# Four edits to the instruction order and buffer placement of a one-core transformer layer: where the feed-forward operands lie, who sums sequence 2's first weights, and what the table splits and casts stand behind

## The chip, the core and the metric

The kernel runs on one core of one Trainium2 chip. Its time is device microseconds of that core. Before the change the median of three runs is 2102.57 us (2102.38 to 2103.07). Engines are named as the profile names them: PE multiplies matrices (PEld is its weight load), DVE is VectorE, ACT is ScalarE, POOL is GpSimd, and SP issues most of the transfers.

## The reference, cut to what matters

Two sequences of 1024 rows and 1024 columns go through one encoder layer. Each has its own conditioning vector, from which six modulation vectors come.

```
h   = rmsnorm(x, g_mix) * (1 + sc1) + sh1
z   = h @ w_in                                 # query latent 256, key/value latent 128, rotary key 64, Fourier input 512
y1  = attention(latents), 4 heads              # full softmax over 1024 keys
y2  = real(fft2(Fourier input)) @ w_four       # over rows and over 64 columns in 8 groups
x   = x + ga1 * (concat(y1, y2) @ w_out)
h2  = rmsnorm(x, g_ffn) * (1 + sc2) + sh2
x   = x + ga2 * ((silu(h2 @ w_gate) * (h2 @ w_up)) @ w_down)     # inner width 2816
out = rmsnorm(x, g_final)
```

All of it is float32 in and out. The kernel keeps float32's accuracy by splitting each operand into a high and a low part: a cast on ACT gives the high part, a subtraction on DVE the low part, and three matmuls (high by high, high by low, low by high) replace one. The helper `split` (lines 62 and 63) is that cast and that subtraction, and `mm3` (lines 78 to 80) is the three matmuls. So nearly every operand passes ACT and DVE before PE can use it.

## The kernel before, in words

**Stages.** Stage 1 walks over eight pairs of row blocks (`pair`, four of each sequence). A pair normalizes and transposes its rows (`norm`, `flip`), multiplies them by the latent weights (`zproj`), transposes the latents (`latents`) and multiplies sums and differences of rows by the folded Fourier weights (`fourier_in`, `evenodd`). Behind the last pair the cosine table `tb[0]` is split. Stage 2 does the Fourier transform over rows (`dft`) with the cosine table `tb[0]` and the sine table `tb[1]`, and multiplies by the output weights that `prep_wm` casts (`fourier_out`). Stage 3 is attention: 64 items, each of one sequence, a block of 256 rows, a head and a half block (`scores`, `flip_p`, `values`), with the next block's queries (`load_q`, `rope_q`, `absorb_q`) and the output projection of an earlier block (`out_step`, `out_proj`, `norm2`, `flip_h`) between them. Stage 4 is the feed-forward part.

**The feed-forward part.** Its products are done by a seven-product scheme of two-by-two blocks: seven combinations of the four blocks of an operand, seven products, and sums of products. `prep_h` splits the seven combinations of h2 (`H[0]`, `H[5]` and so on) into resident tiles, two for each (`H00` and `H01` are the high and the low part of combination 0). `combos(n)` loads the gate and up weights of inner block n into a tile `rgu` and `sums_w` makes their combinations by four subtractions, t3, b12, t2 and t4, all on POOL except for the first two of sequence 1. The loop over n runs seven steps `step(j, ...)`, each a product of twelve matmuls; after step j the weight combination j of the next n is split by `hl` (a `wh` and a `wl` tile, eight buffers of each). The products add up in three banks x, y, z, which `nc.scalar.copy(p1, x)` (line 1397), `add(u2, y, p1, ...)` and later sums read (their helper is line 138). Behind that, `prod2` multiplies by the down weights, and `rows_out` normalizes and stores output rows as a list of seven small steps; for sequence 1's last rows that list is `pending`, and sequence 2's loop over n takes a step from it at two places in each n.

**What sets the order.** The order in each engine's queue is written by a scheduler while the kernel is built. It takes the source order, looks ahead, and is bound by explicit marks: `tc.issue_after(i)` keeps what stands inside it behind instruction i on its engine, `behind()` does so for the cast and the subtraction of the last `split`, and `first(early, late)` sets one order. Within an engine the instructions then run in that order, and one that waits holds all behind it.

**Where tiles lie.** A pool hands out addresses in the order in which tags are first asked for. Stage 4's resident tiles (pool `p5`, tags such as `H00`, `H41`, `X0`, `X1`) are laid over the memory of stage 3. A tile can be written only when the last reader of what lay there has finished. In the kernel before, tag `H41` lies over stage 3's `lat01` (last used by `comb_h`'s result) and tag `H00` over `ckv0` and `ckv1`, the values that the last `values` reads. `H41` first serves as `wc`, the target of the first four weight sums.

**The tail of stage 3.** After the last item, `out_proj(1, 2, ...)` alternates with the last `flip_p` and `values`. Then `out_proj(1, 3, ...)` and two norms and transpositions run between `prep_h`'s steps, ahead of the first feed-forward product. The two `gb` banks that `out_proj` and `values` share come free by DVE (line 938 adds the projection to `x2`).

Of the kernel before, what the change touches and what calls it, by code (L numbers as in the profile page):

```python
# [16 lines left out]
ALU = mybir.AluOpType  # L17
# [35 lines left out]
def hybrid_encoder_kernel(ctx: ExitStack, tc: tile.TileContext, a: dict):  # L53
    nc = tc.nc

    here = {}
# [4 lines left out]
    def split(hi, lo, src):  # L61
        here["a"] = nc.scalar.copy(hi, src).ins  # L62
        here["v"] = nc.vector.tensor_tensor(out=lo, in0=src, in1=rd(hi), op=ALU.subtract).ins  # L63
# [100 lines left out]
    with ExitStack() as st:  # L164
# [378 lines left out]
        def pair(k):  # L543
            if k == 0:
                return first_pair()
            zproj(k, 0)
            if k + 1 < nk:
                flip(k + 1, 0)
                flip(k + 1, 1)
            next(more, None)  # L550
            zproj(k, 1)
            latents(k, 0)
            if k + 1 < nk:
                flip(k + 1, 2)
                flip(k + 1, 3)
            if k + 2 < nk:
                x_load(k + 2)
            next(more, None)
            fourier_in(k, 0)
            latents(k, 1)  # L560
            next(more, None)
            fourier_in(k, 1)
            if k + 1 < nk:
                evenodd(k + 1)
            if k + 2 < nk:
                norm(k + 2)
# [12 lines left out]
        raws = {}  # L579
# [3 lines left out]
                nc.sync.dma_start(raws[k, c][:, :n], a["tcos" if k == 0 else "tsin"][:, c, :])  # L583
        tb[0] = [wr.tile([P, 4, NT], F32R, name=f"tb0{i}") for i in range(2)]
        pair(nk - 1)
        for c in range(4):
            split(tb[0][0][:, c, :], tb[0][1][:, c, :], raws[0, c])

    S = {}

# [106 lines left out]
    with ExitStack() as st:  # L697
# [149 lines left out]
        zsplit(0)  # L847
        nyq_split()
        tb[1] = [wa.tile([P, 4, 512], F32R, name=f"tb1{i}") for i in range(2)]
        for c in range(4):  # L850
            split(tb[1][0][:, c, :], tb[1][1][:, c, :], raws[1, c][:, :512])
        abn = dft(0)
        prep_wm(0)
        zsplit(1)
        scT = wa.tile([P, NC, 32], F32, name="scT2")
        nc.sync.dma_start(scT, sc_d)
# [23 lines left out]
        for s in range(2):  # L880
            for j in (1, 2, 3, 0):
                with tc.issue_after(S.pop("ld")) if (s, j) == (1, 1) else ExitStack():
                    fourier_out(s, abn, j)
                if (s, j) == (1, 1):
                    gate_wo(1, None, here["st"])
                if s == 1 and j == 2:
                    ex = tiny.tile([P, 1], F32, name="ex")
                    nc.vector.memset(ex, 0.0)
                    with tc.issue_after(here["a"]):
                        nc.scalar.activation(ex, ex, AF.Exp)  # L890
                    for u in range(2):
                        rope_q(0, 0, u, bank2)
                if s == 1 and j == 3:
                    absorb_q(0, 0, 0, bank2)
                    for u in range(2):
                        rope_flip(0, 0, u, bank2t)
                if s == 0:
                    n = (1, 2, 3, 0).index(j)
                    mod2(2 * n)
                    mod2(2 * n + 1)  # L900
            if s == 0:
                mr = wa.tile([P, 512], F32, name="modrow2")
                nc.vector.tensor_copy(mr, chunks.pop("ps"))
                abn = dft(1)
                prep_wm(1)
                mod_vecs(mr, bank2, bT, gT, 24, 1, s2, sh2)
                early.close()
                E3 = ExitStack()
                e = E3.enter_context(tc.tile_pool(name="p3e", bufs=1, side="left", reuse_waits="tile"))
                wq_h, wq_l, rc, rs = stage3_loads(gate_wo, rd(abn[1][1][:, 1, 0:1]))  # L910
# [65 lines left out]
    with ExitStack() as st:  # L976
# [104 lines left out]
        for k in range(nit + 4):  # L1081
            if k >= nit:
                i = k - nit
                out_proj(1, 2, i // 2, i % 2)
                S["tail", i] = here["v"]
                if i == 1:
                    norm2(1, 2, 0, tl)
                    S["tail", 5], S["tail", 6] = here["n"]
            if k < nit:
                s, b, h, u = items[k]  # L1090
                scores(s, b, h, u)
                nxt = items[k + 8 - k % 8] if k + 8 - k % 8 < nit else None
                i = k % 8
                if nxt is not None:
                    if i == 0:
                        load_q(*nxt[:2])
                    if i == 3 and nxt[1] == 0:
                        load_seq(nxt[0], w)
                    if i in (3, 4):
                        rope_q(*nxt[:2], i - 3, gbank)  # L1100
                    if i in (5, 6):
                        rope_flip(*nxt[:2], i - 5, tbank)
                if u == 1 and k + 1 < nit:
                    absorb_q(*items[k + 1][:3], gbank)
            if 0 <= k - 1 < nit:
                flip_p(*items[k - 1])
                if k == nit:
                    S["tail"] = here["a"], here["v"]
            if 0 <= k - 3 < nit and (k - 3) % 2 == 1:
                values(*items[k - 3][:3])  # L1110
                if k == nit + 2:
                    S["tail", 4], S["tail", 7] = here["v"], here["a"]
            m = k - 11
            if 0 <= m < 8 * NOUT:
                out_step(*divmod(m // 8, 4), m % 8)
                if m % 8 in (1, 3) and k + 1 < nit:
                    S["late"] = here["n"][1]
            for f in todo.get(k, ()):
                f()

    with ExitStack() as st:
# [6 lines left out]

        def quad(tag, dt=F32):
            return w.tile([P, 4, 512], dt, tag=tag, name=tag, bufs=1)  # L1130

        def prep_h(H, s, n):

# [147 lines left out]
        for s in range(2):  # L1281
            def combos(n, first=False):
                f = order[n]
                if first and n == 1:
                    b = [val() for _ in range(4)]
                    for i, t in enumerate(b):
                        nc.sync.dma_start(t, a["wgu"][i // 2, f][:, 4 * (i % 2) : 4 * (i % 2) + 4, :].rearrange("p c m -> p (c m)"))
                    return b
                r = w.tile([P, 2, 1024], F32, tag=f"X{n % 2}", name="rgu", bufs=1)
                for i in range(2):  # L1290
                    nc.sync.dma_start(r[:, i, :], a["wgu"][i, f])
                return sums_w([r[:, 0, :512], r[:, 0, 512:], r[:, 1, :512], r[:, 1, 512:]], lambda i: val(), nc.gpsimd)

            def comb_h(s, c):
                a11, a21, a12, a22 = (val() for _ in range(4))
# [64 lines left out]
            for n, f in enumerate(order):  # L1360
# [10 lines left out]
                def step(j, ps, k, first, src=src):  # L1371
                    prod(ps, k, cur[j], first)
                    if s == 0 and n == 0:
                        if j == 0:
                            cur.extend(hl(v) for v in w0[4:])
                            w0.clear()
                            norm3(1, S.pop("jk3").bitcast(BF16))
                        if j < 3:
                            with behind():
                                for _ in range(2):  # L1380
                                    next(prep, None)
                            return
                        if j == 3:
                            src = S["w1"] = sums_w(src, lambda i: val(), nc.vector)
                        src = S["w1"]
                        for i in ((), (), (), (0, 1), (2, 3), (4,), (5, 6))[j]:
                            nxt.append(hl(src[i]))
                    elif src is not None:
                        nxt.append(hl(src[j]))
                    if s == 0 and n == 1 and j == 2:  # L1390
                        S.pop("w1", None)
                        flip2(3, [S.pop(("xn", 1, 3, u)) for u in range(2)], bank, lambda g: val())

                x, y, z = bank(), bank(), bank()
                step(0, x, 0, True)
                p1 = val()
                nc.scalar.copy(p1, x)  # L1397
                if pending:
                    with behind():
                        pending.pop(0)()  # L1400
                step(1, y, 5, True)
                u2 = val()
                add(u2, y, p1, nc.vector)
                step(2, x, 1, False)
                sg = val()
                nc.scalar.activation(sg, x, AF.Silu)
                if pending:
                    with behind():
                        pending.pop(0)()
                step(3, y, 6, False)  # L1410
                u3 = val()
                add(u3, y, p1, nc.vector)
                step(4, z, 4, True)
                add(u3, z, u3, nc.vector)
                step(5, y, 3, False)
                add(p1, y, p1, nc.vector)
                nc.scalar.activation(p1, p1, AF.Silu)
# [299 lines left out]
```

## Time and profile before

| what | value |
|---|---|
| median of three runs | 2102.57 us |
| profiled execution | 2103.97 us |
| its span, first to last instruction | 2102.2 us |
| granted PE clock over the span | 0.99 |
| PE busy | 2035.1 us (97%) |
| DVE busy | 1403.6 us (67%) |
| ACT busy | 902.3 us (43%) |
| POOL busy | 832.7 us (40%) |

A share says how much of the span an engine worked, and not what made the others wait. The rows used later are of three kinds: who waited for whom (engine, line, tile, releaser, microseconds in total, number of waits, longest), the order of time (start, duration, engine, line, output and inputs, and in brackets the idle time before it and what ended it), and busy time by stretch with the clock that PE was granted.

### The profile page before, as it was taken

What the parts mean: (1) busy time and instruction counts of PE and PEld (TensorE: products, weight loads), DVE (VectorE), ACT (ScalarE), POOL (GpSimd) and SP (SyncE); (2) the same over time, 40 slices, a digit from 0 to 9 for tenths busy, and PEclk for the clock granted to TensorE, in tenths of its full rate; (3) what the DMA queues carried; (4) which work ended last, traced back from release to release, by engine and by line L of the source; (5) the groups of instructions that cost most, each with busy time, mean ns of one, the idle gap of its engine ahead of it and who ended that gap; (6) DMA issues with size and microseconds to landing.
All of it is one profiled execution on the core that took longest, in us unless ns stands there. A gap on an engine that the chain in (4) does not pass through costs nothing. (4 is left out here: it accounts for less than half of the span.)

```text
span 2102.2 us, 28839 instructions
## 1 busy us (share of the span) xinstructions
PE 2035.1 (97%) x10044; PEld 1667.4 (79%) x10044; DVE 1403.6 (67%) x2088; ACT 902.3 (43%) x1764; POOL 832.7 (40%) x1027
## 2 busy tenths in 40 slices
PE   6999999999999989999999999999999999999998
PEld 3788777888888877888888888877788888888876
DVE  3657766766777667767677666776756566567674
ACT  2766534455555555233323355453233233336441
POOL 1555111111313314878778610334554454420142
PEclk8999999999999999999999999999999999999999
DMA  9685795544643465455455487674332232258672
GB/s 370 206 260 172 258 314 174 131 101 101 157 109 125 146 212 203 165 185 193 168 180 197 159 269 261 212 238 160 116 125 101 76 126 100 76 167 284 226 227 93
DMA packets 187103, 375.49 MB, mean 179 GB/s; under 512 B 19341, under 2 KB 60941, under 8 KB 183885
## 3 DMA queue, kind: packets, MB, share of 16 engines
q1 hardware_dynamic: 168460, 316.09, 45.1%
q0 software_dynamic: 18496, 57.55, 9.1%
q8 instruction: 79, 1.29, 0.3%
q14 instruction: 68, 0.55, 0.1%
HBM read 259.47 MB, written 122.49 MB: 182 GB/s over the span
## 5 line engine op out<-in xcount | busy, mean ns | idle before, releaser
L78 PE MATMUL bank<-H,wh 128*128 128x512 f32 x1232 | 492.7, 400 | 9.2 <-ACT val L1397 4.5
L80 PE MATMUL bank<-H,wl 128*128 128x512 f32 x1232 | 486.7, 395 | 1.9 <-DVE wl L63 1.9
L79 PE MATMUL bank<-H,wh 128*128 128x512 f32 x1232 | 485.0, 394 | 0.2 <-DVE H L63 0.2
L138 DVE TENSOR_TENSOR val<-bank,val 128x512 f32<-128x512 f32 x244 | 167.0, 689 | 194.9 <-PE bank L80 188.0
L78 PEld LDWEIGHTS bank<-H,wh 128*128 128x128 f32 x1232 | 232.0, 188 | 66.1 <-DVE val L138 5.9
L80 PEld LDWEIGHTS bank<-H,wl 128*128 128x128 f32 x1232 | 232.1, 188 | 62.4 <-DVE wl L63 2.6
L79 PEld LDWEIGHTS bank<-H,wh 128*128 128x128 f32 x1232 | 231.8, 188 | 55.7 <-DVE H L63 0.6
L63 DVE TENSOR_TENSOR wl<-draw,wh 128x512 fp32r<-128x512 f32 x286 | 201.9, 741 | 87.5 <-ACT wh L62 87.0
L62 ACT CAST wh<-draw 128x512 fp32r<-128x512 f32 x286 | 168.4, 619 | 159.9 <-PE bank L79 83.8
L138 POOL TENSOR_TENSOR val<-val 128x512 f32<-128x512 f32 x58 | 84.1, 1456 | 368.3 <-DVE val L1498 189.2
L79 PE MATMUL bank<-wl,wh 128*128 128x512 f32 x572 | 223.8, 391 | 3.2 <-DVE wl L63 3.2
L62 ACT CAST wh<-rgu 128x512 fp32r<-128x512 f32 x172 | 106.7, 621 | 270.7 <-PE bank L79 214.2
L78 PE MATMUL bank<-wh 128*128 128x512 f32 x572 | 222.7, 389 | 0.0
L80 PE MATMUL bank<-wh,wl 128*128 128x512 f32 x572 | 222.7, 389 | 0.0
L62 ACT CAST wh<-val 128x512 fp32r<-128x512 f32 x133 | 82.3, 622 | 279.3 <-PE bank L79 250.9
L63 DVE TENSOR_TENSOR wl<-val,wh 128x512 fp32r<-128x512 f32 x133 | 137.8, 1038 | 89.1 <-ACT wh L62 89.0
L135 POOL TENSOR_TENSOR val<-rgu 128x512 f32<-128x512 f32 x84 | 124.2, 1478 | 124.9 <-DMA rgu<-in_wgu_dram 105.4
L63 DVE TENSOR_TENSOR wl<-rgu,wh 128x512 fp32r<-128x512 f32 x172 | 165.3, 962 | 4.8 <-ACT wh L62 4.6
L79 PEld LDWEIGHTS bank<-wl,wh 128*128 128x128 f32 x572 | 107.3, 188 | 28.7 <-DVE wl L63 6.8
L78 PEld LDWEIGHTS bank<-wh 128*128 128x128 f32 x572 | 107.4, 188 | 23.0 <-ACT wh L62 0.3
L80 PEld LDWEIGHTS bank<-wh,wl 128*128 128x128 f32 x572 | 107.4, 188 | 21.9
L135 POOL TENSOR_TENSOR val<-val 128x512 f32<-128x512 f32 x89 | 120.1, 1366 | 1.3
(354 smaller groups left out, 4053.4 us busy)
## 6 DMA issues: line engine op xcount, KB each, us to landing
rgu<-in_wgu_dram SPq DMA_DIRECT2D x86, 512.0 KB
draw<-s_d SPq DMA_DIRECT2D x143, 256.0 KB
s_d<-val POOLq DMA_DIRECT2D x88, 256.0 KB, 4.0
draw<-t_d SPq DMA_DIRECT2D x88, 256.0 KB
s_d<-val SPq DMA_DIRECT2D x66, 256.0 KB
draw<-in_w_down_dram SPq DMA_DIRECT2D x55, 256.0 KB
wada<-in_w_ada_dram SPq DMA_DIRECT2D x13, 1024.0 KB
xt<-in_x_dram SPq DMA_DIRECT2D x16, 512.0 KB
```

The costliest lines, as they stand in the source:

```text
L62: here["a"] = nc.scalar.copy(hi, src).ins
L63: here["v"] = nc.vector.tensor_tensor(out=lo, in0=src, in1=rd(hi), op=ALU.subtract).ins
L78: nc.tensor.matmul(out, lh, rh, start=first, stop=False, skip_group_check=cont)
L79: nc.tensor.matmul(out, lh, rl, start=False, stop=False, skip_group_check=cont)
L80: here["t"] = nc.tensor.matmul(out, ll, rh, start=False, stop=last, skip_group_check=cont).ins
L135: return eng.tensor_tensor(out=out, in0=x, in1=y, op=ALU.subtract).ins
L138: eng.tensor_tensor(out=out, in0=x, in1=y, op=ALU.add)
```

## The change

1. **Placement.** A loop at the head of stage 4 asks for the sixteen resident tags in a written order. In the built program two tags change places by it, and no other tile moves: `H00` lies where `H41` lay (over `lat01`) and `H41` lies where `H00` lay (over `ckv0` and `ckv1`).
2. **Sequence 2's first weight sums.** `combos(0)` sums on DVE. `combos(1)` of sequence 2 only loads; its sums are made on DVE in step 2 of n = 0, behind the sum u2, and the splits of n = 1's weights stand behind the copy of p1. A third place in each n takes a step from `pending`.
3. **Tables and casts.** The four splits of `tb[0]` stand behind the split of the last pair's first latents. The four splits of `tb[1]` stand behind the previous split, and all of `prep_wm(0)` stands behind the last of them.
4. **Queries.** `load_q(0, 1)`, the load of stage 3's second query block, moves from the first item of stage 3 into stage 2, ahead of eight stores of `fourier_out`.

```diff
@@ pair
             latents(k, 0)
+            here["l0"] = here["a"], here["v"]
@@ end of stage 1
         pair(nk - 1)
-        for c in range(4):
-            split(tb[0][0][:, c, :], tb[0][1][:, c, :], raws[0, c])
+        with tc.issue_after(here["l0"][0]), tc.issue_after(here["l0"][1]):
+            for c in range(4):
+                split(tb[0][0][:, c, :], tb[0][1][:, c, :], raws[0, c])
@@ stage 2
-        for c in range(4):
-            split(tb[1][0][:, c, :], tb[1][1][:, c, :], raws[1, c][:, :512])
+        with behind():
+            for c in range(4):
+                split(tb[1][0][:, c, :], tb[1][1][:, c, :], raws[1, c][:, :512])
+        mk = here["a"], here["v"]
         abn = dft(0)
-        prep_wm(0)
+        with tc.issue_after(mk[0]), tc.issue_after(mk[1]):
+            prep_wm(0)
@@
                 if s == 1 and j == 2:
+                    load_q(0, 1)
@@ stage 3
-                    if i == 0:
+                    if i == 0 and k > 0:
                         load_q(*nxt[:2])
@@ stage 4
+        for tag in ("H20", "X0", "X1", "H21", "H30", "H31", "H00", "H41", "H01", "H50", "H51", "H10", "H11", "H40", "H60", "H61"):
+            quad(tag)
@@ combos
-                return sums_w([r[:, 0, :512], r[:, 0, 512:], r[:, 1, :512], r[:, 1, 512:]], lambda i: val(), nc.gpsimd)
+                b = [r[:, 0, :512], r[:, 0, 512:], r[:, 1, :512], r[:, 1, 512:]]
+                return b if n == 1 and s == 1 else sums_w(b, lambda i: val(), nc.vector if n == 0 else nc.gpsimd)
@@ step
+                    elif s == 1 and n == 0:
+                        if j == 2:
+                            with tc.issue_after(here["u2"]):
+                                S["w1"] = sums_w(src, lambda i: val(), nc.vector)
+                        with behind(), tc.issue_after(here["c"]) if j > 1 else ExitStack():
+                            for i in ((), (), (0,), (1, 2), (3,), (4,), (5, 6))[j]:
+                                nxt.append(hl(S["w1"][i]))
+                        if j == 6:
+                            S.pop("w1")
@@ the loop over n
+                def pend():
+                    if pending:
+                        with behind():
+                            pending.pop(0)()
-                nc.scalar.copy(p1, x)
+                here["c"] = nc.scalar.copy(p1, x).ins
-                if pending:
-                    with behind():
-                        pending.pop(0)()
+                pend()
-                add(u2, y, p1, nc.vector)
+                here["u2"] = nc.vector.tensor_tensor(out=u2, in0=y, in1=p1, op=ALU.add).ins
...
                 add(u3, z, u3, nc.vector)
+                pend()
```

More of the change, by code (lines that the diff above doesn't have):

```diff
@@ L1406, in hybrid_encoder_kernel @@
                 nc.scalar.activation(sg, x, AF.Silu)
-                if pending:
-                    with behind():
-                        pending.pop(0)()
+                pend()
                 step(3, y, 6, False)
@@ L1414, in hybrid_encoder_kernel @@
                 add(u3, z, u3, nc.vector)
+                pend()
                 step(5, y, 3, False)
```

## The prediction, made before the changed kernel had run

> **What bounds the kernel now.** I read the page's engine shares first, then PE's waits, then the granted clock by stretch, then the order of time at the five places that the change touches.
>
> ```profile
> span 2102.2 us, 28839 instructions
> PE 2035.1 (97%) x10044; PEld 1667.4 (79%) x10044; DVE 1403.6 (67%) x2088; ACT 902.3 (43%) x1764; POOL 832.7 (40%) x1027
> ```
>
> PE works 97% of the span. The change removes no matmul, so all it can win is PE's idle time, 2102.2 − 2035.1 = 67 us, and time in which PE works at a lower clock.
>
> ```profile
> PE bank L78 <- ACT val L1397: 4.5, 2, 3.1
> PE gb L78 <- DVE x L938: 4.1, 1, 4.1
> PE bank L78 <- DVE val L138: 4.1, 2, 2.1
> PE gb L80 <- DMA ql<-lat_d: 2.5, 1, 2.5
> PE bank L438 <- DVE lat L423: 2.3, 2, 2.1
> PE bank L80 <- DVE wl L63: 1.9, 2, 1.4
> ```
>
> These are PE's waits beside the change (engine, line, releaser, then microseconds in all, number, longest). None is a lack of work on PE: each is one instruction held on another engine. Four lie where the source is edited: the latents (L438), the query load (ql), the projection into the `gb` bank (L938), and sequence 2's first products (L1397, L138).
>
> ```profile
> 334.51:337.92 3.41, 0.93 (x6) 0.72 (x5) 1.59 (x5) 1.54 (x3) 0.00 (x0) 1.00 0.97 305
> 337.92:341.33 3.41, 3.41 (x15) 2.94 (x14) 2.21 (x5) 0.54 (x1) 0.72 (x1) 0.50 0.85 312
> 764.58:767.99 3.41, 1.48 (x4) 1.19 (x5) 2.15 (x4) 3.03 (x5) 1.72 (x6) 0.50 0.30 71
> 767.99:771.41 3.42, 3.42 (x10) 2.65 (x9) 3.32 (x6) 0.00 (x0) 0.00 (x0) 0.50 0.64 235
> 798.72:802.13 3.41, 1.31 (x6) 1.05 (x6) 3.41 (x5) 3.12 (x4) 0.00 (x0) 1.00 0.06 23
> 802.13:805.54 3.41, 3.41 (x9) 2.65 (x8) 3.38 (x6) 0.01 (x1) 0.00 (x0) 0.50 0.01 2
> 1450.66:1454.07 3.41, 3.41 (x10) 2.40 (x8) 3.41 (x7) 0.28 (x1) 0.00 (x0) 0.50 0.48 148
> ```
>
> The columns are the stretch, its length, busy time of PE, PEld, DVE, ACT and POOL, and then the granted clock. A stretch of 3.41 us in which PE worked 0.93 or 1.31 us is followed by one at clock 0.50. So an idle gap is paid twice: once as idle, and then as half of the PE time in the slow stretch. After 337.92 that is 3.41 / 2 = 1.7 us, after 764.58 (1.48 + 3.42) / 2 = 2.5 us, after 802.13 and after 1450.66 1.7 us each.
>
> **Part 1, placement.**
>
> ```profile
> 762.42 1.99 ACT L62 CAST H<-H 128x1024 fp32r<-128x1024 f32 x2 [7.91 <-PE gb L80]
> 763.50 2.36 DVE L63 TENSOR_TENSOR H<-H,H 128x1024 fp32r<-128x1024 f32 x2 [5.93 <-ACT H L62]
> 765.77 0.68 DVE L938 TENSOR_TENSOR x<-x,gb 128x512 f32<-128x512 f32 x1
> 766.51 0.80 PE L78 MATMUL gb<-wv,o0b 128*128 128x512 f32 x1 [4.13 <-DVE x L938]
> 771.83 0.69 DVE L938 TENSOR_TENSOR x<-x,gb 128x512 f32<-128x512 f32 x1 [0.25 <-PE gb L80]
> 776.65 0.75 DVE L948 TENSOR_SCALAR xn<-x,rs_r 128x1024 f32<-128x1024 f32 x1 [1.26 <-POOL rs_r L109]
> 777.11 0.27 PE L1209 MATMUL pht<-ident,xn 128*128 128x128 f32 x1
> ```
>
> The cast into `H00` stands idle 7.91 us until PE's last read of `ckv` ends. DVE waits for that cast, and the addition at L938 stands behind DVE's two subtractions. That addition would free the `gb` bank, so PE waits 4.13 us for an addition that needs nothing from `ckv`. In the built program the cast into `H00` now waits for `comb_h`'s transfers instead, and the weight sums, which now go over `ckv`, wait for PE.
>
> With the same durations: the two casts start at 762.42 − 7.91 = 754.5, everything behind them moves 7.9 earlier, and the subtractions end at about 758 and the addition at 766.45 − 7.9 = 758.6, before PE asks for the bank at 766.51 − 4.13 = 762.38. The gap goes (4.1) and so do its two slow stretches (2.5): 6.6 at most. The sums start behind `ckv`'s last read at about 763.2 instead of 768.7 and are not late. What is late next is the norm behind the projection: PE finishes it at 765.1 (twelve matmuls of 0.227, below, behind 762.38), the sums (four at about 0.7) hold the addition to 766.7, and the chain from there to `xn` took 776.65 − 771.83 = 4.8 us before, so `xn` is ready at 771.75 while PE comes to its transposition (777.11 before, less 6.4) at 770.7. A new wait of about 1.0 stays. I take 5.6, with ends 3.0 (PE waits again for another addition behind the sums) and 6.6.
>
> **Part 2, sequence 2's first sums.**
>
> ```profile
> 1438.08 1.29 POOL L135 TENSOR_TENSOR val<-rgu 128x512 f32<-128x512 f32 x1 [14.83 <-DMA rgu<-in_wgu_dram]
> 1448.61 1.60 POOL L135 TENSOR_TENSOR val<-rgu,val 128x512 f32<-128x512 f32 x1
> 1448.56 0.62 ACT L62 CAST wh<-val 128x512 fp32r<-128x512 f32 x1 [2.68 <-POOL val L135]
> 1442.81 0.50 PE L78 MATMUL bank<-H,wh 128*128 128x512 f32 x1 [0.36 <-ACT wh L62]
> 1449.72 0.50 PE L78 MATMUL bank<-H,wh 128*128 128x512 f32 x1 [3.06 <-ACT val L1397]
> 1490.60 2.44 DVE L1524 SCALAR_TENSOR_TENSOR val<-val,rs_r,gf 128x512 f32<-128x512 f32 x2
> 1495.87 0.50 PE L78 MATMUL bank<-H,wh 128*128 128x512 f32 x1 [2.00 <-DVE val L138]
> 768.72 0.68 DVE L135 TENSOR_TENSOR H<-rgu 128x512 f32<-128x512 f32 x1
> ```
>
> POOL makes eight sums from 1438.1 to 1450.2. ACT's cast of n = 1's second combination waits for the seventh, and the copy of p1 (L1397) that frees bank x stands behind that cast, so PE waits 3.06 us for data of a later n. On DVE a sum takes 0.68: four take 2.8, n = 0's last combination is there at about 1440.9, ACT's six casts end at about 1443.4, and the copy follows at 1444.0, before PE wants the bank: it came to bank x's last product at 1442.81 − 0.36 = 1442.45, and twelve matmuls (2.7) behind that is 1445.2. The waits of 0.4 (1442.81) and 0.5 (1.9 less 1.4 of the row for L80) in the same steps go too, and so does the slow stretch (1.7). The wait of 2.0 at 1495.87 stands behind two scalings (2.44) of `pending`, which with three steps a round are done before n = 2. At most 0.4 + 0.5 + 3.1 + 1.7 + 2.0 = 7.7.
>
> The cost is on DVE. Eight sums (5.4 us) and a third pending step (an addition and a scaled product, 1.2 to 1.9) come into n = 0. A later round is the measure: in 20 us it has 88 matmuls, 0.227 each, and DVE is busy 16.35. A round of 84 matmuls thus lasts 19.1 us, and with some 7 us more DVE is full. Laid out by hand at 0.6 to 0.7 an operation, DVE frees bank y for step 5 about 0.4 us before PE wants it and bank z for step 6 about 0.6 before. That holds only while POOL leaves DVE alone.
>
> ```profile
> 1443.42 1.74 POOL L135 TENSOR_TENSOR val<-rgu 128x512 f32<-128x512 f32 x1
> 1443.93 1.78 DVE L63 TENSOR_TENSOR wl<-rgu,wh 128x512 fp32r<-128x512 f32 x1
> 1464.00:1484.00 20.00, 20.00 (x88) 16.07 (x87) 16.35 (x23) 7.58 (x15) 10.99 (x17) 1.00 0.40 144
> ```
>
> While POOL sums, a DVE operation on such a tile takes 1.78 instead of 0.68: 1.1 more. POOL's sums for n = 2 will fall at about 1454 to 1460, on DVE's fullest stretch. I take three such operations less 2.0 us of slack at the end of n = 0: 1.4 lost, so 6.3 won. Ends: 2.5 (five more stretched operations reach PE) and 7.7.
>
> [...]
>
> **Part 3, tables and casts.**
>
> ```profile
> 221.50 1.24 ACT L62 CAST tb<-raw 128x514 fp32r<-128x514 f32 x2 [1.74 <-DMA raw<-in_tcos_dram]
> 222.64 0.38 ACT L411 ACTIVATE junk<-bank 128x256 bf16<-128x256 f32 x1
> 225.60 0.48 DVE L423 TENSOR_SCALAR lat<-bank,rs_r 128x256 f32<-128x256 f32 x1 [0.99 <-POOL rs_r L109]
> 226.23 0.41 PE L438 MATMUL bank<-ident,lat 128*128 128x128 f32 x2 [2.07 <-DVE lat L423]
> 234.61 0.39 PE L78 MATMUL bank<-tb,zh 128*128 128x258 f32 x1 [0.98 <-ACT zh L62]
> ```
>
> ACT stood idle from 219.76 to 221.50 for the table's transfer, and the square at L411 behind the two casts waited for nothing of its own. Ahead of them it can start up to 222.64 − 219.76 = 2.9 us earlier, more than the 2.07 that PE waits for the end of that chain. The four casts (0.62 each, 2.5) then run to about 227.5 and their subtractions (half of 1.18 each by the row at 763.50) end by 230; the first transform, at 234.61 before, would need them at 232.4, so they are hidden behind `fourier_in`. If that cover is gone, each further cast costs 0.6. The wait of 0.98 for `zh` is a chain of its own and stays. `prep_wm(0)` behind `tb[1]` is wanted only by the output products behind the transform; I cost it at nothing. I take 2.1; ends 0 (the next wait takes all) and 2.3 (both waits of L438).
>
> **Part 4, queries.** The two loads now stand ahead of eight stores in SP's queue, so the 2.5 us wait and its slow stretch (1.7) go: 4.2 at most. The eight stores stand behind two issues more; nothing reads them before attention's output projection. Next in line is DVE:
>
> ```profile
> 345.00:357.00 12.00, 11.35 (x75) 9.87 (x74) 11.58 (x26) 7.84 (x16) 0.74 (x1) 1.00 0.01 1
> ```
>
> There DVE works 11.58 of 12 us while PE waits little, so part of what PE wins it waits for again. I take 3.2; ends 1.5 and 4.2.
>
> **Sum.** 5.6 + 6.3 + 2.1 + 3.2 = 17.2 us, in span and execution alike. The profiled execution is 2103.97, so 2086.8; the median of runs is 1.4 lower, so 2085.4. All low ends together give 7.0, all high ends 20.8.
>
> **Rivals.** A) *DVE becomes the bound in sequence 2's first rounds.* The place is n = 0 and n = 1, where DVE is filled. The price is 1.1 for each operation that POOL stretches. It decides against the change when about (17.2 + 2.0) / 1.1 = 18 operations beyond those counted reach PE. Against it: POOL has only four large sums in that stretch and each can hold about one DVE operation. If 20 reached PE, the time would be 2085.4 + 22 − 2 = 2105. Chance 0.05. A milder form, part 2 at its low end and part 4 too, gives 2085.4 + 3.8 + 1.7 = 2091; chance 0.13.
>
> B) *Placement does not do what it says*: another release holds the cast or the addition, and part 1 brings nothing. For it: the cast now waits for POOL's transfers. Against: POOL's queue is idle long before 754. Time 2085.4 + 5.6 = 2091; chance 0.06.
>
> C) *The slow stretches fall elsewhere.* The longer of the two waits for L138 (2.1), which no edit mends, lies in one 3.41 us stretch of the clock's grid before (798.72 to 802.13). It moves some 11 us earlier (parts 1, 3 and 4), which is not a multiple of 3.41, and where two stretches share it neither need be low: 1.7 more won, 2083.7. Chance 0.22. [...]
>
> D) *Parts 3 and 4 are given back*, as transfers are busy 0.97 of the stretch at 334.51: 2085.4 + 2.1 + 3.2 = 2091; chance 0.05.
>
> My forecast itself, 2085.4, has 0.49; its own range is 2082 to 2089.
>
> **How the numbers follow.** C to D lie between 2083 and 2091; the low end of the range takes C with parts 1, 2 and 4 at their high ends, 2083.7 − 1.0 − 1.4 − 1.0 = 2080, the high end takes the milder A and B, 2092. A measurement tells 0.2% (4.2 us) from no change, so faster means under 2098.4. Only A, and mishaps not named, lie above: faster 0.92, same 0.03, slower 0.05.
>
> **What would show it.** Part 1: no PE wait for L938 over 1 us, and a wait of about 1 us before L1209. Part 2: no wait for L1397 over 0.5 us, and PE waits for L138 in n = 0 or n = 1. Part 3: no wait for L423 over 0.5. Part 4: no wait for `ql`. Clock 0.50 in one or no stretch between 330 and 2090. Wrong: DVE full from 1445 to 1475 with PE waits of several us there.

## The result, and the profile after

The changed kernel takes 2084.54 us in the median of five runs (2083.05 to 2087.97), beside 2102.57 us for the kernel before in five runs of its own (2101.01 to 2103.11): a ratio of 0.9920 with a 95% interval of 0.9909 to 0.9931. The forecast was 2085.4 us. The profiled execution is the one of 2084.54 us.

The head of its page, with the span and the first row of busy times:

```profile
span 2082.8 us, 28834 instructions
PE 2028.8 (97%) x10044; PEld 1662.8 (80%) x10044; DVE 1409.5 (68%) x2096; ACT 901.9 (43%) x1764; POOL 824.6 (40%) x1019
```

The span is 19.4 us shorter. PE was busy 6.3 us less with the same 10044 matmuls, since fewer of them ran at half clock (ahead of the kernel's tail ten stretches at clock 0.50 before and five now, of these five and four in the first 55 us); the other 13.1 us are idle time of PE that is gone. PE's waits in the changed kernel, of those beside the edits and in the feed-forward part (engine, line, releaser, microseconds in all, number, longest; line 944 was 938, 1219 was 1209, 1422 was 1397 and 1426 is u2's sum, split off from the helper at 138):

```profile
PE bank L79 <- DVE wl L63: 2.7, 5, 0.9
PE bank L78 <- ACT val L1422: 1.6, 1, 1.6
PE bank L80 <- DVE wl L63: 1.4, 1, 1.4
PE bank L78 <- ACT zod L62: 1.0, 1, 1.0
PE bank L78 <- ACT zh L62: 1.0, 1, 1.0
PE bank L78 <- DVE val L1426: 1.0, 1, 1.0
PE pht L1219 <- DVE xn L954: 0.9, 1, 0.9
PE bank L80 <- DVE B L63: 0.6, 1, 0.6
PE bank L78 <- DVE val L138: 0.5, 1, 0.5
```

There is no row for the `gb` bank and `x`, none for `ql`, none for L438 and `lat` from DVE. The four waits at which the edits aim are gone. The copy of p1 still has one row (L1422, 1.6); that wait stands in sequence 1's second round, where the kernel before waited too.

Laid beside each other matmul by matmul, the two traces show where the 19.4 us came from: 0.5 in the start-up, 2.3 at the latents, 0.5 given back at the wait for `B`, 3.7 at the queries and just behind, 0.8 given back in the middle of attention (a wait of 0.9 us for `p` that no edit touches; the second trace of the kernel before has it too, with 0.97), 6.6 at the projection, 0.7 given back at the transposition behind it, 1.1 in the first feed-forward round of sequence 1, and 7.2 in sequence 2's first three rounds.

The end of attention in the order of time:

```profile
749.26 2.00 ACT L62 CAST H<-H 128x1024 fp32r<-128x1024 f32 x2
752.36 2.35 DVE L63 TENSOR_TENSOR H<-H,H 128x1024 fp32r<-128x1024 f32 x2
754.63 0.68 DVE L944 TENSOR_TENSOR x<-x,gb 128x512 f32<-128x512 f32 x1
757.10 0.40 PE L78 MATMUL gb<-wv,o0b 128*128 128x512 f32 x1
760.82 0.68 DVE L944 TENSOR_TENSOR x<-x,gb 128x512 f32<-128x512 f32 x1
766.44 0.33 PE L1219 MATMUL pht<-ident,xn 128*128 128x128 f32 x1 [0.86 <-DVE xn L954]
```

Up to here the changed kernel is 5.2 us ahead (2.3 − 0.5 + 3.7 − 0.8 and the start-up's 0.5). The casts into `H00` start at 749.26, which is 754.4 on the clock of the kernel before, and not at 762.42: they no longer wait for the last read of `ckv`. The addition that frees the `gb` bank (754.63) is done at 755.3, so PE starts the projection at 757.10 with no wait where it had waited 4.13 us. The next addition (760.82) stands behind the weight sums, and the new wait is where the prediction put it: 0.86 us ahead of the transposition of `xn`.

Sequence 2's first rounds, at the same times in both traces (the changed kernel is 12 to 18 us further on in the program there), by stretch (the stretch, its length, busy time of PE, PEld, DVE, ACT and POOL, the granted clock), before and after:

```profile
1436.00:1456.00 20.00, 15.99 (x60) 11.55 (x59) 13.21 (x14) 7.68 (x15) 12.83 (x12) 0.91 0.34 123
```

```profile
1436.00:1456.00 20.00, 20.00 (x87) 15.82 (x85) 19.96 (x27) 8.00 (x16) 12.71 (x18) 1.00 0.33 118
```

DVE went from 14 operations in 20 us to 27 and is busy 19.96 of 20, as full as rival A feared, and PE never waits there.

### The profile page after: what moved, and what is told of

Same layout as the page of the kernel before. It is cut to its first block, busy times and chain, and to the rows that moved or that the text cites. A ratio compares the mean times of both kernels' runs of the same rounds, so it can differ in the third digit from the quotient of the medians.

```text
span 2082.8 us, 28834 instructions
## 1 busy us (share of the span) xinstructions
PE 2028.8 (97%) x10044; PEld 1662.8 (80%) x10044; DVE 1409.5 (68%) x2096; ACT 901.9 (43%) x1764; POOL 824.6 (40%) x1019
## 3 DMA queue, kind: packets, MB, share of 16 engines
q8 instruction: 79, 1.29, 0.3%
## 4 chain that ended last, share of the span: by engine, by line
PE 54%; DVE 2%; DMA 2%; POOL 2%; issue 1%; ACT 1%; SPq 0%; DVEq 0%; POOLq 0%; ACTq 0%
PE bank L80 18%; PE bank L78 18%; PE bank L79 18%; DMA val<-x_d 1%; DVE wl L63 1%; DMA draw<-t_d 1%; POOL val L138 1%; DMA rgu<-in_wgu_dram 1%; DVE val L138 1%; DVE val L1546 0%; ACT wh L62 0%; POOL val L135 0%; DVE H L63 0%; DMA draw<-s_d 0%; POOL rs_y L105 0%
## 5 line engine op out<-in xcount | busy, mean ns | idle before, releaser
L138 DVE TENSOR_TENSOR val<-bank,val 128x512 f32<-128x512 f32 x200 | 136.5, 688 | 157.4 <-PE bank L80 152.2
L138 POOL TENSOR_TENSOR val<-val 128x512 f32<-128x512 f32 x58 | 82.6, 1432 | 368.5 <-DVE val L1520 188.4
L135 POOL TENSOR_TENSOR val<-rgu 128x512 f32<-128x512 f32 x80 | 118.3, 1478 | 107.4 <-DMA rgu<-in_wgu_dram 86.1
L1004 DVE TENSOR_REDUCE mx<-ps_s 128x1 f32<-128x1024 f32 x64 | 78.2, 1221 | 63.7 <-PE ps_s L999 63.5
```

Of the source, the lines that this page charges most:

```text
L135: return eng.tensor_tensor(out=out, in0=x, in1=y, op=ALU.subtract).ins
L138: eng.tensor_tensor(out=out, in0=x, in1=y, op=ALU.add)
L1004: nc.vector.tensor_reduce(out=mx, in_=ps, axis=AX.X, op=ALU.max)
```

## The experiments

Every kernel here computes the whole layer. Each was timed in five rounds beside the kernel before on the same chip unless it says otherwise, and the interval is that of the ratio.

**1. Each edit alone.** The kernel before, with one of the four edits as the diff above has it.

> The kernel before with edit 1 alone (the written order of the sixteen tags; H00 and H41 change places, nothing else moves). My theory: the cast into H00 no longer waits for PE's last read of ckv, the wait of 4.13 us for L938 and its two slow stretches go, a wait of about 1 us stays ahead of the transposition of xn: 5.6 us won (3.0 to 6.6), 2097.0. Rival, clock: what the gap cost beyond its 4.13 us comes back where the next waits fall (a slow stretch behind the first feed-forward waits, as in the changed kernel at 778): 3.5 to 4.1 won, 2098.5 to 2099. Rival, placement does nothing: within 1 us of before.

> The kernel before with edit 2 alone (sequence 2's first sums on VectorE, casts behind the copy of p1, a third place for pending). My theory: 6.3 us won (2.5 to 7.7), 2096.3; the waits of 0.36, 0.52, 3.06 and 2.00 us and one slow stretch go, about 0.5 us of new waits for L138. Rival A: VectorE becomes the bound there and PE waits several us between 1435 and 1490: less than 2.5 won or a loss.

> The kernel before with edit 3 alone (table splits behind the last latents, output-weight casts behind the sine table). My theory: the wait of 2.07 us for L423 goes: 2.1 won (0 to 2.3), 2100.5. Rival D, given back: the changed kernel shows a new wait of 0.57 us for a low part of B, so 1.5 or less is won, and the later wait for ql may grow by what was won here (0 won at the end of the span).

> The kernel before with edit 4 alone (the second query block's load moved into stage 2, ahead of eight stores). My theory: the wait of 2.48 us for ql and the slow stretch behind it go: 3.2 won (1.5 to 4.2), 2099.4. Rival D: VectorE, busy 11.58 of 12 us behind it, hands part of it on as waits: under 1.5 won. Additivity: if the four alone sum to the 18.0 of the whole within 2 us, the edits do not touch each other; a sum that is far off means that they do.

| kernel | median us (before: 2099.83) | change | ratio, 95% interval |
|---|---|---|---|
| placement alone | 2093.85 | −6.0 | 0.9966 (0.9957 to 0.9976) |
| sums alone | 2091.07 | −8.8 | 0.9959 (0.9946 to 0.9973) |
| tables alone | 2097.99 | −1.8 | 0.9989 (0.9980 to 0.9997) |
| queries alone | 2100.50 | +0.7 | 1.0004 (0.9994 to 1.0014) |

Placement gives what was forecast (5.6), and its interval (5.0 to 9.0 us) leaves out the 3.5 to 4.1 of the clock rival. Tables give 1.8 where 2.1 was forecast, but the interval (0.6 to 4.2 us) holds rival D's 1.5 as well, and the trace has a wait of 1.47 us for `B` in exchange for the one for `lat`. The sums give more than the 6.3, though the interval (5.7 to 11.3 us) holds it. The queries give nothing: the interval reaches from 1.3 us won to 2.9 us lost, and the 3.2 us lie outside it. The four add up to 15.9 us, between the 18.0 us above and the 13.8 of the whole on another chip (experiment 2), so nothing shows that the edits touch each other.

In the trace of the queries alone the wait for `ql` is gone, and another wait of the same kind has come, well ahead of anything that this edit moves. PE's row, and the ACT row at its root:

```profile
254.30 0.50 PE L80 MATMUL bank<-wm,B 128*128 128x512 f32 x1 [1.90 <-DVE B L63]
```

```profile
244.27 0.73 ACT L784 ACTIVATE wm<-wraw,cmask 128x512 fp32r<-128x512 f32 x1 [2.39 <-DMA wraw<-wm_d]
```

ACT waited 2.39 us for an output-weight transfer, and `B`'s low part came late behind it; a slow stretch follows. In the first trace of before that row has 0.52 us of such a wait, a few us later, and PE none. So transfers in stage 2 land now early, now late, and this moves PE's waits from one execution to the next, in these two by 1.90 us.

**2. The whole once more, and without edit 4.** Only the order of SP's queue differs between the two.

> The changed kernel once more, beside the kernel before on this chip. If each edit gives what the first pair of traces showed (1.8 tables, 3.7 queries, 5.8 placement, 7.2 sums): 18 us won again. If the query wait of 2.48 us was the luck of one execution's transfers (1.15 and 0.31 us in two later traces whose program is unchanged there, and no slow stretch behind them): 15 to 16 won.

```diff
                 if s == 1 and j == 2:
-                    load_q(0, 1)
...
-                    if i == 0 and k > 0:
+                    if i == 0:
                         load_q(*nxt[:2])
```

> The changed kernel with edit 4 undone: the two loads stand behind eight stores again, and only the order of SP's queue differs. As predicted (the wait and its slow stretch): 3.2 to 4.2 us more than the changed kernel. Transfer luck: a wait for ql of 0.3 to 1.2 us without a slow stretch, so 0 to 1.2 more.

On a third chip the whole gives 2085.65 against 2099.48 us, 13.8 us: 0.9938 (0.9924 to 0.9951), or 10.3 to 16.0 us. The 18 us of the first pair of traces lie outside that, and 15 to 16 at its upper end. Without edit 4 it is 2087.69, 0.9948 (0.9935 to 0.9960), 2.0 us more, with intervals that overlap by more than half; and its trace has no wait of 0.3 us or more for `ql`, so the 2.0 cannot be put down to that wait. That trace is of the slowest of its five executions, and what it has beyond the changed kernel's is a wait of 2.96 us for the copy of p1 at 830.9 us, in sequence 1 (1.59 and 1.40 in the changed kernel's two traces), with two slow stretches behind it. Those two waits for `ql` that two single-edit traces still had (their releaser rows; 1.15 us with placement alone, 0.3 with the sums alone) were followed by no slow stretch. The changed kernel itself repeats to 1.1 us on the two chips; it is the kernel before that stood 3 us higher on the first.

**3. The kernel before once more,** one profiled execution.

> The kernel before once more, for its trace on this chip. If the query wait of 2.48 us belongs to the program: about 2.5 again. If it was transfer luck: anything from 0 to 2.5. The waits that engines cause (2.07, 4.13, 3.06, 2.00) repeat within 0.3 us; whether a slow stretch follows each depends on where the clock's grid falls.

One time, 2100.84 us. The waits that engines cause came back: 2.13 us for `lat`, 4.13 for `x`, 2.96 for the copy of p1, 1.98 for L138. The wait for `ql` did not: nothing of 0.3 us or more. Of the ten traces whose program has the loads in their old place, `ql` cost PE 2.48, 1.15 and 0.31 us in three and under 0.2 in the other seven, this one among them. The 2.48 us that the prediction priced were the transfer luck of the execution that it read.

**4. Is it the order on ACT?** The kernel before, with the copy of p1 ahead of the two casts that wait for POOL.

```diff
-                nc.scalar.copy(p1, x)
+                here["c"] = nc.scalar.copy(p1, x).ins
...
+                    elif s == 1 and n == 0 and j < 2:
+                        if j == 1:
+                            with tc.issue_after(here["c"]):
+                                nxt.extend(hl(v) for v in src[:2])
```

> The kernel before with one order on ACT: in sequence 2's n = 0 the casts of n = 1's first two combinations stand behind the copy of p1; all sums stay on POOL and pending keeps two places. If the wait of 3.06 us was the copy held behind a cast that waits for POOL, as I argued: that wait and the slow stretch go, 3 to 4.8 us won of the 8.8 that edit 2 measured, and the wait of 2.00 us for L138 stays. If VectorE's faster sums are what counted: under 1 won, and a wait as long moves to a weight of n = 1.

2100.92 against 2099.48 us, 1.0006 (0.9997 to 1.0015): nothing won. PE in that round:

```profile
1448.58 0.50 PE L78 MATMUL bank<-H,wh 128*128 128x512 f32 x1 [4.38 <-DVE val L138]
```

The wait for the copy is gone and a longer one stands in its place, for u2's sum on DVE. The mechanism as I had put it, a copy held behind a cast, names the last link only. Two traces of experiment 1 whose program is that of before in this round show both links late at once: PE waits 2.23 us for the copy and then 1.63 for u2's sum with placement alone, 2.50 and 1.63 with queries alone.

**5. Is it the order on both engines?** The kernel before, with casts and subtractions of n = 1 behind the copy and behind u2's sum.

```diff
+                    elif s == 1 and n == 0:
+                        with tc.issue_after(here["c"]) if j > 1 else ExitStack(), tc.issue_after(here["u2"]) if j > 1 else ExitStack():
+                            for i in ((), (), (0,), (1, 2), (3,), (4,), (5, 6))[j]:
+                                nxt.append(hl(src[i]))
...
```

> The kernel before with two orders: in sequence 2's n = 0 the splits of n = 1's weights stand behind the copy of p1 on ACT and behind the sum u2 on VectorE (casts and subtractions alike, on the steps that edit 2 gives them); all sums stay on POOL, pending keeps two places. With the copy alone ahead, PE waited 4.38 us for the sum u2, which stood behind a subtraction that waits for POOL. If what held PE was the order on both engines: no wait over 1 us from 1440 to 1452, 4 to 5.5 us won. If POOL's late sums hold PE wherever they are put: the wait moves on to u3 or to a weight of n = 1, under 1.5 won.

2100.17 against 2100.19 us, 1.0000 (0.9991 to 1.0009). Order alone wins nothing here either. The trace of this kernel, in the order of time:

```profile
1439.37 1.76 POOL L135 TENSOR_TENSOR val<-rgu 128x512 f32<-128x512 f32 x1
1439.89 1.78 DVE L63 TENSOR_TENSOR wl<-rgu,wh 128x512 fp32r<-128x512 f32 x1
1441.21 1.63 POOL L135 TENSOR_TENSOR rgu<-rgu 128x512 f32<-128x512 f32 x1
1441.21 0.57 ACT L1401 COPY val<-bank 128x512 f32<-128x512 f32 x1
1441.60 1.78 DVE L63 TENSOR_TENSOR wl<-val,wh 128x512 fp32r<-128x512 f32 x1
1443.31 1.77 DVE L63 TENSOR_TENSOR wl<-rgu,wh 128x512 fp32r<-128x512 f32 x1
1445.01 1.76 DVE L63 TENSOR_TENSOR wl<-val,wh 128x512 fp32r<-128x512 f32 x1
1446.69 0.68 DVE L63 TENSOR_TENSOR wl<-rgu,wh 128x512 fp32r<-128x512 f32 x1
1448.61 0.68 DVE L1407 TENSOR_TENSOR val<-bank,val 128x512 f32<-128x512 f32 x1
1449.35 0.50 PE L78 MATMUL bank<-H,wh 128*128 128x512 f32 x1 [3.92 <-DVE val L1407]
```

The copy is done at 1441.8 and the casts of n = 0's weights stand ahead of it, so nothing on DVE between 1439.9 and 1446.7 waits for late data. These are five of n = 0's own subtractions, and four of them take 1.76 to 1.78 us, beside POOL's sums of n = 1's weights; the fifth takes 0.68. Four times 1.1 is 4.4 us of DVE. PE waits 3.92 us for u2's sum, which stands behind them and behind two operations of `pending` (1.3 us). The kernel before has the same four rows (1.78, 1.78, 1.75, 1.75 from 1443.9 on) beneath its wait for the copy.

What edit 2 won is thus read as POOL's sums taken out of DVE's way, more than POOL's late data. Of late data there is some: from n = 0's first sum to its second subtraction it is 4.7 us here, with the sums on POOL (1434.03 to 1438.74), and 2.9 in the changed kernel, with the sums on DVE (1424.81 to 1427.71), so 1.8 beside the 4.4. A kernel in which POOL leaves DVE alone and makes the sums all the same was not tried, so the split between the two stays a reading.

That the longer subtractions go with POOL's sums is seen on both engines in the trace of before:

```profile
1442.18 1.27 POOL L135 TENSOR_TENSOR val<-rgu,val 128x512 f32<-128x512 f32 x1
1442.79 1.22 DVE L63 TENSOR_TENSOR wl<-val,wh 128x512 fp32r<-128x512 f32 x1 [5.20 <-ACT wh L62]
1446.93 1.59 POOL L135 TENSOR_TENSOR val<-rgu 128x512 f32<-128x512 f32 x1
1447.33 1.75 DVE L63 TENSOR_TENSOR wl<-rgu,wh 128x512 fp32r<-128x512 f32 x1
1450.68 1.28 DVE L63 TENSOR_TENSOR wl<-rgu,wh 128x512 fp32r<-128x512 f32 x2
```

POOL's four sums of 128x512 from 1438.08 on, three of them while DVE stood idle, take 1.27 to 1.29 us each; the next four, beside DVE's subtractions, take 1.59 to 1.74. The last of them ends at 1450.21, and the two subtractions from 1450.68 on take 1.28 us together. Why the operations of the two engines lengthen together no run shows.

**6. Edit 2 without its third place for `pending`.**

```diff
                 add(u3, z, u3, nc.vector)
-                pend()
                 step(5, y, 3, False)
```

> Edit 2 alone without its third place for pending. If the wait of 2.00 us for L138 in the third round is pending's scalings standing ahead of the sum, as I argued: it returns, and this is 2.0 us slower than edit 2 alone (3.7 with a slow stretch behind the wait), 5 to 6.8 won against the kernel before instead of 8.8. If not: no difference over 1 us.

2094.10 against 2100.19 us, 6.1 won, 0.9974 (0.9966 to 0.9983), beside 8.8 with the third place. The wait for L138 two rounds later is back, with a slow stretch behind it:

```profile
1485.83 0.50 PE L78 MATMUL bank<-H,wh 128*128 128x512 f32 x1 [1.84 <-DVE val L1416]
```

So about 2.7 of edit 2's 8.8 us belong to the third place, and about 6 to the sums and their order. The two intervals overlap, since each is taken against the kernel before; that the wait itself comes and goes is what the traces show.

**7. Edit 3 without the mark on the output-weight casts.**

```diff
-        with tc.issue_after(mk[0]), tc.issue_after(mk[1]):
-            prep_wm(0)
+        prep_wm(0)
```

> Edit 3 alone without its last mark, so the output-weight casts are free to go early as before. I costed that mark at nothing: the same as edit 3 alone within 1 us, 1 to 2.5 won. If the wait for the low part of B (0.57 to 1.47 us in three traces with the mark) comes from the mark: that wait is gone and 0.6 to 1.5 us more is won. Against it: the same wait stands at 1.90 and 0.77 us in two traces without the mark.

2099.69 against 2100.19 us: 1.0002 (0.9993 to 1.0010), hardly anything is left of the 1.8. The two intervals still share 0.9993 to 0.9997, so that the mark is worth something is likely and not beyond doubt. PE's wait for `zod` in this kernel and with the mark:

```profile
PE bank L78 <- ACT zod L62: 2.7, 1, 2.7
```

```profile
PE bank L78 <- ACT zod L62: 1.0, 1, 1.0
```

ACT's rows ahead of that wait, without the mark:

```profile
235.74 0.62 ACT L62 CAST wm<-wraw 128x512 fp32r<-128x512 f32 x1 [1.25 <-DMA wraw<-wm_d]
236.27 0.40 ACT L62 CAST zod<-zo 1x256 fp32r<-1x256 f32 x1
```

With the table casts out of the way, the scheduler lets output-weight casts go early, and one that waits for its transfer holds `zod`: PE waits 1.7 us more, works 1.05 of that stretch's 3.42 us, and the next stretch is at clock 0.50. The order is the program's; the 1.25 us at its root are a transfer's, seen in one execution, so how much is paid on the mean is not known.

The wait for `B` does not need the mark, since two of the nine traces without it have one (0.77 and 1.90 us). But four of the five with it do (0.57, 0.83, 0.95 and 1.47), and this kernel has none. Whether the mark makes that wait more frequent stays open.

**8. Two more orders of the same kind.** The changed kernel, with two casts of sequence 1's second round behind the copy of p1, and the second half of one H tile behind the first weight splits.

```diff
                 wts = [hl(w0[i]) for i in range(2)]
-                next(prep, None)
+                with behind():
+                    next(prep, None)
...
+                    elif s == 0 and n == 1 and j < 2:
+                        if j == 1:
+                            with tc.issue_after(here["c"]):
+                                nxt.extend(hl(v) for v in src[:2])
```

> The changed kernel with two more orders of the same kind: sequence 1's n = 1 casts its first two weights of n = 2 behind the copy of p1 (a wait of 1.59 us for that copy), and the cast and subtraction of H[5]'s second half stand behind the first two weight splits (a wait of 1.38 us for wl and the slow stretch behind it). By the reading of the waits: 1.6 + 1.4 + up to 1.7 = 3.0 to 4.7 less than the changed kernel. If the next instruction is then late: under 1.5 less.

2083.60 us, against 2085.65 for the changed kernel on the same chip: 0.9927 (0.9915 to 0.9939) beside 0.9938 (0.9924 to 0.9951). It has the lowest median of all, but the intervals overlap, a gain over the changed kernel is not shown, and the 2.05 us between the medians lie between the two answers that were expected. In its trace the waits of 1.38 and 1.59 us are gone. This has come in, and behind it the wait for L138 (0.98 in the changed kernel's first trace) is 2.11 us at 788.4, with a slow stretch:

```profile
781.06 0.50 PE L78 MATMUL bank<-H,wh 128*128 128x512 f32 x1 [0.82 <-ACT val L1427]
```

## Why the prediction was right, point by point

The time lay 0.9 us under the forecast and well inside the range. Placement was right with its mechanism. Tables and sums were right within their intervals, each with a step that failed or is in doubt, and queries was read off an accident. That the sum came out so close is in part luck: errors of opposite sign, and in the pair of traces 0.5 + 1.1 − 0.8 us at places that no edit touches. The 17.2 us lie inside the first measurement's interval (14.5 to 19.1 us won) and outside that of experiment 2 (10.3 to 16.0).

- **Placement, 5.6 forecast.** Right: 6.0 alone, 6.6 less 0.7 in the trace of the whole. The step that named what is late next, the norm behind the projection with about 1.0, measured 0.86. (The prediction's own 766.7 + 4.8 is 771.5 and not 771.75, so that step should have said 0.8.)
- **Sequence 2's sums, 6.3 forecast.** 8.8 alone, 7.2 in the trace of the whole. The wait of 2.00 behind `pending`'s scalings was right (experiment 6). The step "ACT's cast of n = 1's second combination waits for the seventh, and the copy of p1 that frees bank x stands behind that cast" failed as an explanation: with that cast moved away PE waited 4.38 us, and with the subtractions moved away too 3.92. Beneath it, as experiment 5 is read, lay the 1.1 us by which each of four DVE operations took longer beside POOL's sums (1.78 us and not 0.68), which the prediction had measured and then charged only to the cost of the edit, not to the kernel before. That cost was oversized as well. In the changed kernel POOL's sums for n = 2 fall from 1442.9 to 1449.4 and stretch four operations, by 3.5 us together. Three of them, and ahead of the last a sum with one input in a bank, which kept its 0.68 us while POOL worked (on a sum from 1446.03 to 1447.67):

```profile
1443.33 1.46 DVE L63 TENSOR_TENSOR wl<-rgu,wh 128x512 fp32r<-128x512 f32 x1
1444.71 1.78 DVE L138 TENSOR_TENSOR val<-val 128x512 f32<-128x512 f32 x1
1446.43 0.68 DVE L138 TENSOR_TENSOR val<-bank,val 128x512 f32<-128x512 f32 x1
1448.14 1.78 DVE L63 TENSOR_TENSOR wl<-rgu,wh 128x512 fp32r<-128x512 f32 x1
```

  The forecast had three, by 3.3 us, of which 1.4 would reach PE (3.3 − 2.0 is 1.3), and its low end of 2.5 is three and a half more of them at 1.1, not five. In those rounds PE waits 0.50 us (the row for L138 above). Rival A needed eighteen more and found one.
- **Tables, 2.1 forecast.** Right in sum, 1.8 alone, and the wait for `lat` is gone from every trace with the edit. The step that cost the mark on `prep_wm(0)` at nothing is in doubt: without the mark the one trace has 1.7 us more of the wait for `zod` with a slow stretch, and the edit wins next to nothing, at the edge of the noise. Rows for it stood in the trace of before, where output-weight casts wait for `wraw`; I looked at what the mark delays and not at what it keeps from going early.
- **Queries, 3.2 forecast.** Mis-sized: +0.7 alone (1.3 won to 2.9 lost), because the wait of 2.48 us was there in one execution and not in most. "So the 2.5 us wait and its slow stretch (1.7) go" is true of the two traces that were compared, and of few others.
- **Rival B** did not come: no wait for L938 (now L944) is left. **Rival D** came in part: behind the latents the wait for `B` gives back 0.57 and 0.95 us in the changed kernel's two traces, and 1.47 with tables alone; part 4 had little to give.
- **Rival C** came as a mechanism, and not as a gain. In the changed kernel the wait of 1.38 us at 776 falls with other short ones into one stretch of the grid, and the next is slow:

```profile
774.83:778.25 3.42, 1.80 (x7) 0.91 (x7) 3.42 (x6) 3.39 (x7) 0.65 (x1) 1.00 0.88 259
778.25:781.66 3.41, 3.41 (x10) 2.65 (x9) 2.72 (x5) 3.02 (x5) 2.35 (x2) 0.50 0.80 323
```

  While PE ran at half clock, DVE caught up (busy 2.72 of 3.41 us), so the wait for L138 behind it shrank from 2.10 to 0.98 us and its own slow stretch stayed away. In the second trace of the changed kernel it is the other way round: no slow stretch at 777, 2.10 us at 788.6 and a slow stretch at 790.6. The trace without edit 4 goes as the first (a slow stretch at 779.1, then a wait of 1.00 us). In these three, what is won at one of them is paid at the other.

As forecast, one slow stretch is left between 330 us and the kernel's tail (at 778.25 us); the clock falls once more, to 0.50, at 2075, where it fell at 2096 before, as the last products end.

## What to carry to other kernels

A wait's releaser row names the link that came last. Before an order is mended for it, look one engine further back, at whether its neighbours run at their undisturbed durations. Here the copy stood behind a late sum of POOL, and the next sum on DVE behind four subtractions that took 1.76 to 1.78 us beside POOL's sums, and not 0.68: mending one order brought out the other, and taking that work away won what no order did. A wait for a transfer that stands in one trace is to be seen in a second before it is priced; the wait of 4.13 us between engines came back to the hundredth in all nine traces that have it, the one for `ql` ran from 0 to 2.5. And before a mark that delays work is costed at nothing, look at what it keeps from going early, which the queue without it shows.

## What the runs showed of the hardware that I had not expected

The price of an idle gap depends on where it falls on the clock's grid. That there is such a grid is read from the slow stretches: in the trace of before they start at 337.92, 802.13 and 1450.66 us, which are 136 and 190 times 3.413 us apart. The same 4.13 us wait, in the kernel with the copy first and in the kernel before once more (stretches as above):

```profile
759.60:763.02 3.42, 0.00 (x0) 0.00 (x0) 2.96 (x3) 3.42 (x6) 0.87 (x2) 1.00 0.00 0
763.02:766.43 3.41, 3.41 (x8) 2.73 (x9) 2.17 (x4) 1.10 (x2) 0.85 (x5) 0.50 0.84 293
766.43:769.84 3.41, 3.41 (x16) 2.82 (x16) 3.34 (x6) 1.11 (x3) 0.65 (x1) 1.00 0.04 14
```

```profile
759.40:762.82 3.42, 1.42 (x13) 1.22 (x11) 0.88 (x1) 1.96 (x3) 0.00 (x0) 1.00 0.02 7
762.82:766.23 3.41, 1.28 (x3) 1.10 (x4) 2.14 (x4) 3.23 (x6) 1.72 (x6) 0.50 0.22 68
766.23:769.64 3.41, 3.41 (x9) 2.67 (x9) 3.31 (x6) 0.00 (x0) 0.00 (x0) 0.50 0.63 240
```

Where the gap empties one stretch (0.00 us of PE's work), one slow stretch follows, by its clock 3.41 / 2 = 1.7 us lost; where it is split (1.42 and 1.28 us), both halves count, and two follow, of which the first is more than half idle itself: (1.28 + 3.41) / 2 = 2.3 us lost. Over the fourteen traces of this case, between 200 and 2050 us, each of the 41 stretches in which PE worked under 0.47 of the time was followed by one at clock 0.50; of ten between 0.49 and 0.53, two were; of some 7500 above, three, and all three stood in a slow stretch already. So a gap need not fill a stretch of 3.41 us: the wait of 1.98 to 2.00 us for L138 behind `pending` was followed by a slow stretch in two traces of five. The bound that these counts show is on the share of a stretch in which PE works, near half.
